# A two-layer decoder trunk on one core: a set of token sums one chunk pair later, and convolution steps held back while a seven-product chunk pair runs

## The chip, the core and the metric

The kernel runs on one core of a Trainium2 chip. The engines are named as the profile names them: PE multiplies matrices (PEld is its weight load), DVE is the vector engine, ACT the scalar engine, POOL and SP mostly issue DMAs. Each engine takes its instructions in a fixed order. The metric is the device time of one execution in microseconds (us), as a median over runs.

## The reference: what is computed

The trunk has two layers over 256 tokens of width 2048. Layer 0 mixes by gated linear attention, layer 1 by forgetting attention; both end in the channel mixer `conv_ffn`, which is where the change lies:

```
def causal_dwconv(u, w, b):
    s_ = u.shape[1]
    up = jnp.pad(u, ((0, 0), (CONV_WIDTH - 1, 0), (0, 0)))
    return w[0] * up[:, 0:s_] + w[1] * up[:, 1:s_ + 1] + w[2] * up[:, 2:s_ + 2] + b

def conv_ffn(h, w_up, conv_w, conv_b, w_down):
    u = causal_dwconv(h @ w_up, conv_w, conv_b)
    a, val = split_cols(u, [FFN_HIDDEN, FFN_HIDDEN])
    return (jax.nn.silu(a) * val) @ w_down
```

`w_up` is 2048 x 11264 and `w_down` 5632 x 2048, all in float32.

## The kernel before

**Products.** A float32 product is made of three passes of a rounded type: each operand is split into a high part (`hi`, a rounding copy) and a low part (`lo`, the rest), and hi x hi, lo x hi and hi x lo are added up in PSUM. Weights come from memory in units (`raw`, one DMA each, issued by SP). For every unit `split_unit` (lines 210 to 230) has ACT write `whi` (L229) and DVE write `wlo` (L230). There are four buffers each of `raw`, `whi` and `wlo`, so these engines can be at most four units ahead of PE.

**Wide panels.** `pair_steps` (from L363) runs one panel of 1024 output columns over chunks of 128 rows of the weight. An ordinary chunk is one unit: two blocks of tokens by two halves of columns, 12 matmuls of 128 x 512. Two neighbouring chunks whose token sums have been prepared are run as a **seven-product pair**: by a scheme of the Strassen kind the 2 x 2 x 2 block product takes seven products, 21 matmuls, instead of eight, 24. The pair has weights `ra` and `rb` (two DMAs into `raw2`), from which four weight blocks are split: `w1` (half of `ra`), `w2` (`rb`), and after four subtractions on DVE (L427 to L430) `w3` (`ra`, needs L427 and L428) and `w4` (`rb`, needs L429 and L430). `split_more` does the splits: ACT at L377, DVE at L378. The products are named p1 to p7; p1 uses w1, p2 and p3 use w2, p5 and p7 use w3, p6 and p4 use w4. When the last pair of a panel is done, `early` takes the finished banks out; its first step is an ACT copy of p1 (L1321 in the down projection, L1471 in the up projection), which waits for PE to finish p1, and in the down projection a DVE addition to the stream `x` (L485) follows on it.

**Token sums.** The sums of tokens and chunks that the seven products need are made by `token_sums` (four additions or subtractions on DVE, then a split on ACT and DVE, L671 and L672). For the up projection they are made once, for chunk 6 (`SEVEN_UP`), and for the first panel after each change of part also for chunk 11 (`SEVEN_MORE`). For the down projection they are made when the gated rows of certain chunks are finished: the table `SEVEN_DOWN` (L36) names chunk and buffer.

**Order of the work.** The 44 chunks of the hidden width go in three parts, 0 to 15, 16 to 27 and 28 to 43 (`PARTS`). An up panel (`up_pair`) makes four chunks of hidden rows; a down panel uses up the rows of a part. The up panels of a part come first, with one up panel of the next part ahead of the down panels. In the last part the first down panel is the one called `wide` below: it runs 12 of its 16 chunks, then three units of the narrow panel `f2`, then the last four chunks, whose hidden rows come last.

**Convolution steps.** The result of an up panel goes to memory and back in another layout (`far_away`, by POOL's DMAs) and is then convolved in small steps: 12 taps on ACT (L1383), two additions on DVE (L1390), the activation on ACT (L1396), the gating on DVE (L1403) and two splits (L515 on ACT, L516 on DVE). Each step has a cost in credits (0.5 per tap, 1.0 for an addition and so on, 10.2 for a half panel of two chunks). `pair_steps` yields once per chunk, twice after a seven-product pair; at each yield the driving loop calls `tick(share)`, which adds `share` credits and hands out due steps until the credit is used up. `drive` gives 1.3 credits per yield in up panels and in the other down panels, the loop over `wide` and `f2` gives 2.1. A step handed out is placed behind the latest weight split that was written (`issue_after(casts[-1])` or `lows[-1]`), and a scheduler that works on a model of the times then lays down the order on every engine.

Of the kernel before, what the change touches and what calls it, by code (L numbers as in the profile page):

```python
# [32 lines left out]
PARTS = ((0, 16), (16, 28), (28, 44))  # L33
RING = 20
SEVEN_UP = (6,)
SEVEN_DOWN = {4: 0, 10: 1, 20: 0, 32: 1}  # L36
SEVEN_MORE = 11


# [78 lines left out]
def _layout():  # L118

    where, off = {}, 0  # L120
    for key, _, kcs, cols, per in _panels():
        n = sum(c[1] for c in cols)
        units = []
        for u in range(0, len(kcs), per):
            units.append((off, kcs[u : u + per], n))
            off += P * per * n
        where[key] = units
    return where, off
# [17 lines left out]
def _trunk(ctx: ExitStack, tc: tile.TileContext, xt, xtok, memt, wp, wgu, gns, gfin, cnv, par, msk, out):  # L146
    nc = tc.nc
    where, _ = _layout()
# [232 lines left out]
    def pair_steps(units, src, sums, flip, pool, early, late):  # L381

        bank = {}
        fast, slow = ("p1", "p5", "p7", "p6"), ("p2", "p3", "p4", "x")
        accs, works = (slow, fast) if flip else (fast, slow)
        tags = {n: ("acc", 4) for n in accs}
        tags.update(zip(works, (("o", 1), ("s", 2), ("s", 2), ("t", 1))))
        begun = set()
        sums = dict(sums)
        n = len(units)  # L390
        plan = []
        k = 0
        while k < n:
            plan.append(k)
            k += 2 if k in sums else 1
        end = [k for k in plan if k in sums]

        def mm(name, x, w, last):
            if name not in bank:
                tag, bufs = tags[name]  # L400
                bank[name] = (pacc.tile([P, 512], F32, name="acc", tag="acc") if tag == "acc" else work(tag, bufs))
            r = TE.matmul(bank[name], x, w, start=name not in begun, stop=last)  # L402
            begun.add(name)
            return r

        def tok(k, b):
            return [src[k][:, part, b * P : (b + 1) * P] for part in range(2)]

        def three(name, x, w, last=False):
            for i, (a, b) in enumerate(((0, 0), (1, 0), (0, 1))):  # L410
                r = mm(name, x[a], w[b], last and i == 2)
            return r

        places = (("p2", 0, 0), ("p4", 1, 0), ("p3", 0, 1), ("x", 1, 1))
        for k in plan:
            if k in sums:
                with tc.high_priority(offset=AHEAD):
                    ra, rb = [pool.tile([P, NUNIT], F32, name="raw2", tag="raw2", bufs=2) for _ in range(2)]
                    with tc.issue_after(loads[-1].ins):
                        for t, (off, _, w) in ((ra, units[k]), (rb, units[k + 1])):  # L420
                            loads.append(nc.sync.dma_start(t, wp[off : off + P * w].rearrange("(p n) -> p n", p=P)))
                st = [[sums[k][:, part, j, :] for part in range(2)] for j in (3, 0, 1, 2)]
                done = k == end[-1]
                w1 = split_more(ra[:, :512], 512)
                w2 = split_more(rb, 1024)
                with tc.high_priority(offset=AHEAD):
                    V.tensor_tensor(ra[:, :512], ra[:, 512:], ra[:, :512], ALU.subtract)  # L427
                    V.tensor_tensor(ra[:, 512:], rb[:, 512:], ra[:, 512:], ALU.subtract)  # L428
                    V.tensor_tensor(rb[:, 512:], rb[:, 512:], ra[:, :512], ALU.subtract)  # L429
                    V.tensor_tensor(rb[:, :512], rb[:, :512], rb[:, 512:], ALU.subtract)  # L430
                three("p1", tok(k, 0), [t[:, :512] for t in w1], done)
                three("p2", tok(k + 1, 0), [t[:, :512] for t in w2])
                three("p3", st[3], [t[:, 512:] for t in w2])
                w3 = split_more(ra, 1024)
                three("p5", st[0], [t[:, :512] for t in w3], done)
                three("p7", st[2], [t[:, 512:] for t in w3], done)
                w4 = split_more(rb, 1024)
                three("p6", st[1], [t[:, 512:] for t in w4], done)
                last_mm.append(three("p4", tok(k + 1, 1), [t[:, :512] for t in w4]))
                if done:  # L440
                    early(bank)
                yield k
                k += 1
            else:
                w = split_unit(units[k])
                last = k == n - 1
                steps = [(low, *place) for low in range(2) for place in places]
                if last:
                    steps.sort(key=lambda t: places.index(t[1:]))
                for low, name, b, h in steps:  # L450
                    for part in range(2 - low):
                        r = mm(name, tok(k, b)[part], w[low][:, h * 512 : (h + 1) * 512], last and low == 1)
                    if last and low:
                        ends.append(r)
                        late(b, h, bank[name])
                last_mm.append(r)
            yield k
# [907 lines left out]
    def ffn(l, nx, h, m, ys, zs, landing, then, pool, temps, last=None, spare=None):  # L1365
        with tc.tile_pool(name=f"ffn{l}", bufs=1) as fp:
# [31 lines left out]
            def gated(j, s):  # L1398
# [6 lines left out]
                with tc.issue_after(lows[-1].ins):  # L1405
                    split(m, (j + s) % RING, r[:, s, :])
                    if s and j in SEVEN_DOWN:
                        sums[j] = held("dsum", SEVEN_DOWN[j])
                        token_sums(r, sums[j])
# [39 lines left out]
            def tick(share):  # L1449

                clock[0] += 1
                credit[0] = min(credit[0], 0.0) + share
                while returns and returns[0][0] <= clock[0] and not unread[returns[0][1]]:
                    _, slot, back, steps = returns.pop(0)
                    back()
                    unread[slot] = 12
                    waiting.extend(steps)
                while waiting and waiting[0][0] <= clock[0] and credit[0] > 0:
                    _, cost, step = waiting.pop(0)
                    credit[0] -= cost  # L1460
                    step()
# [27 lines left out]
                 9: lambda: nx.land(landing[1]), 11: nx.take}.get(k, int)()  # L1489
                tick(0)  # L1490

            def drive(steps, share=1.3):
                for _ in steps:
                    tick(share)

            up_sums = {k: input_sums(k) for k in SEVEN_UP}
            for k in up_pair(0):
# [22 lines left out]
            wide = down_pair(l, p, 0, src, {c - lo: t for c, t in sums.items()}, 0, pool, lambda: (temps(0), temps(1)), then)  # L1520
# [10 lines left out]
                f2 = panel_tm(("down", l, p, 2), src, third)  # L1531
                f3 = panel_tm(("down", l, p, 3), src, lambda b, a: (add_to(3)(b, a), then(3, b)))
            last_pair = hi - lo - 4
            for k in range(last_pair):
                next(wide)
                tick(2.1)
            getattr(then, "begin", int)()
            for u in range(3):
                f2(u)
                tick(2.1)  # L1540
            for _ in wide:
                tick(2.1)
            assert not waiting and not returns
            if l:
                for u in range(3, 8):
# [218 lines left out]
```

## Time and profile before

| what | value |
|---|---|
| runs, median (lowest to highest) | 2233.29 us (2229.81 to 2234.18), 3 runs |
| the profiled execution | 2230.85 us |
| its span, first to last instruction | 2229.1 us |
| PE busy | 2211.6 us, 10323 matmuls |
| DVE busy | 1789.9 us |
| ACT busy | 1418.9 us |
| granted PE clock over the span | 0.998 |

A row of the timeline is start, duration, engine, line, operation, the tiles written and read, their shape, a count and, in brackets, how long the engine was idle before it and who ended that. Matmuls are pipelined: a row's duration is longer than the time to the next start, so a loss on PE is read from starts. Names of tiles in the trace have no numbers; in the rows of the order they have.

### The profile page before, as it was taken

Reading aid. Unit: us, or ns where it says so; the run is one execution under the profiler, and the core shown is the slowest. Engines: PE = TensorE matmul, PEld = TensorE weight load, DVE = VectorE, ACT = ScalarE, POOL = GpSimd, SP = SyncE. Lnnn points to the kernel's source line nnn. Section 1 sums busy time; section 2 is a strip of 40 time slices with the busy share of each in tenths; the row PEclk is TensorE's granted clock in tenths of the full one; section 3 lists DMA queues with packets and bytes.
Section 4 is the critical chain, followed back from the end, with each engine's and each line's share of the span. In section 5 each row is a group of like instructions: output and inputs, shape, how many; then the busy total and the mean of one; then the engine's idle time right before and its main releaser. Section 6 shows DMA issues by size and latency. Waiting matters only on the chain.

```text
span 2229.1 us, 30049 instructions
## 1 busy us (share of the span) xinstructions
PE 2211.6 (99%) x10323; PEld 1851.9 (83%) x10323; DVE 1789.9 (80%) x2654; ACT 1418.9 (64%) x2257; POOL 136.0 (6%) x257
## 2 busy tenths in 40 slices
PE   9999999999999999999999999999999999999998
PEld 7888888888788888888788998888888888888876
DVE  7768977688887888898978569678888788888895
ACT  6655664556786567656765455455787657665874
POOL 0000000001100000001010000000001000100100
PEclk9999999999999999999999999999999999999999
DMA  9877567777778567667677867777677757766674
GB/s 348 249 224 224 193 186 245 253 233 242 228 234 267 183 221 238 227 233 233 222 247 250 237 194 249 228 240 249 210 241 238 252 175 246 232 241 209 226 259 146
DMA packets 165633, 515.47 MB, mean 231 GB/s; under 512 B 20700, under 2 KB 41832, under 8 KB 165480
## 3 DMA queue, kind: packets, MB, share of 16 engines
q1 hardware_dynamic: 148488, 461.36, 63.4%
q0 software_dynamic: 16416, 51.40, 7.5%
q8 instruction: 81, 1.33, 0.2%
q10 hardware_dynamic: 576, 0.79, 0.1%
q14 instruction: 72, 0.59, 0.1%
HBM read 469.68 MB, written 43.79 MB: 230 GB/s over the span
## 4 chain that ended last, share of the span: by engine, by line
PE 90%; issue 5%; ACT 2%; DMA 1%; DVE 1%; POOL 0%; SPq 0%; ACTq 0%; DVEq 0%; POOLq 0%
PE acc L333 26%; PE acc L402 25%; PE ps_s L402 13%; PE ps_o L402 7%; PE ps_t L402 6%; PE acc L305 3%; PE acc L260 3%; PE acc L363 2%; PE ps_s L333 2%; PE acc L258 1%; ACT tap L1383 1%; DMA raw<-wp 1%; ACT whi L229 1%; PE ps_s L1010 0%; DMA yzu<-far 0%
## 5 line engine op out<-in xcount | busy, mean ns | idle before, releaser
L230 DVE TENSOR_TENSOR wlo<-raw,whi 128x1024 fp32r<-128x1024 f32 (+4 forms) x739 | 874.1, 1194 | 289.0 <-ACT whi L229 261.9
L229 ACT ACTIVATE whi<-raw 128x1024 fp32r<-128x1024 f32 (+4 forms) x739 | 760.2, 1037 | 432.7 <-PE acc L333 151.2
L333 PE MATMUL acc<-whi,B 128*128 128x512 f32 (+3 forms) x1248 | 291.8, 370 | 0.0
L333 PEld LDWEIGHTS acc<-whi,B 128*128 128x128 f32 x1248 | 227.1, 188 | 28.1
L377 ACT ACTIVATE whi<-raw 128x1024 fp32r<-128x1024 f32 (+1 forms) x136 | 129.7, 954 | 188.8 <-PE ps_t L402 76.4
L378 DVE TENSOR_TENSOR wlo<-raw,whi 128x1024 fp32r<-128x1024 f32 (+1 forms) x136 | 147.6, 1087 | 65.5 <-ACT whi L377 60.7
L402 PE MATMUL acc<-whi,mix 128*128 128x512 f32 x764 | 195.4, 390 | 0.9 <-ACT whi L229 0.8
L402 PE MATMUL acc<-whi,B 128*128 128x512 f32 x750 | 193.0, 390 | 0.5 <-ACT whi L229 0.4
L402 PEld LDWEIGHTS acc<-whi,mix 128*128 128x128 f32 x764 | 143.0, 188 | 32.5 <-ACT whi L229 2.5
L402 PEld LDWEIGHTS acc<-whi,B 128*128 128x128 f32 x750 | 140.6, 188 | 31.0 <-ACT whi L229 1.6
L333 PE MATMUL acc<-wlo,B 128*128 128x512 f32 (+3 forms) x624 | 158.6, 369 | 0.0
L1383 ACT ACTIVATE tap<-yzu,cw 128x256 f32<-128x256 f32 x264 | 124.7, 530 | 4.0 <-DMA yzu<-far 4.0
L333 PEld LDWEIGHTS acc<-wlo,B 128*128 128x128 f32 x624 | 114.5, 188 | 14.6 <-DVE wlo L230 0.2
L1383 ACT ACTIVATE tap<-fvt,cw 128x256 f32<-128x256 f32 x264 | 124.7, 531 | 2.0 <-DMA fvt<-far 2.0
L402 PE MATMUL acc<-wlo,mix 128*128 128x512 f32 x382 | 107.8, 390 | 0.0
L402 PE MATMUL acc<-wlo,B 128*128 128x512 f32 x375 | 107.1, 390 | 0.0
L1390 DVE TENSOR_TENSOR tap<-tap,tap 128x1024 f32<-128x1024 f32 x88 | 106.7, 1213 | 0.0
L402 PE MATMUL ps_s<-whi,mix 128*128 128x512 f32 x386 | 105.2, 389 | 0.0
L402 PE MATMUL ps_s<-whi,B 128*128 128x512 f32 x342 | 94.3, 390 | 0.0
L402 PEld LDWEIGHTS ps_s<-whi,mix 128*128 128x128 f32 x386 | 72.5, 188 | 15.3
L402 PEld LDWEIGHTS acc<-wlo,mix 128*128 128x128 f32 x382 | 71.6, 188 | 15.3 <-DVE wlo L230 0.3
L402 PEld LDWEIGHTS acc<-wlo,B 128*128 128x128 f32 x375 | 70.3, 188 | 15.0 <-DVE wlo L230 0.3
(498 smaller groups left out, 3792.3 us busy)
## 6 DMA issues: line engine op xcount, KB each, us to landing
raw<-wp SPq DMA_DIRECT2D x743, 512.0 KB, 4.5
fvt<-far POOLq DMA_DIRECT2D x100, 128.0 KB, 4.6
raw<-wp SPq DMA_DIRECT2D x32, 384.0 KB, 3.5
far<-yu POOLq DMA_DIRECT2D x22, 512.0 KB, 5.5
far<-yzu POOLq DMA_DIRECT2D x22, 512.0 KB, 5.4
yzu<-far POOLq DMA_DIRECT2D x88, 128.0 KB, 5.2
raw<-wp SPq DMA_DIRECT2D x24, 388.0 KB, 5.2
x<-xtok SPq DMA_DIRECT2D x8, 512.0 KB, 7.3
```

What stands on the lines that cost most here:

```text
L229: casts.append(S.activation(hi[:, s], raw[:, s], AF.Copy))
L230: lows.append(V.tensor_tensor(lo[:, s], raw[:, s], hi[:, s].bitcast(F32), ALU.subtract))
L258: mm = TE.matmul(acc[p][c][:, :T], w[:, s], both[:, 0, :], start=False, stop=end and j == 3)
L260: mm = TE.matmul(acc[p][c], w[:, s], both, start=u == j == 0, stop=end and j == 3)
L305: mm = TE.matmul(acc[b][:, :n], src[kcs[j] - base][:, part, b * P : (b + 1) * P], w, start=u == 0 and low == part == j == 0, stop=u == end ...
L333: mm = TE.matmul(acc[b][:, :n], src[kc - base][:, part, b * P : (b + 1) * P], ready[low][:, j * n : (j + 1) * n], start=i == low == part = ...
L363: mm = TE.matmul(acc[b][:, :n], src[kc - base][:, part, b * P : (b + 1) * P], w, start=i == low == part == j == 0, stop=i == end and low = ...
L377: casts.append(S.activation(hi[:, :n], src, AF.Copy))
L378: lows.append(V.tensor_tensor(lo[:, :n], src, hi[:, :n].bitcast(F32), ALU.subtract))
L402: r = TE.matmul(bank[name], x, w, start=name not in begun, stop=last)
L1383: S.activation(by_run(taps[i][:, s, c, i:]), zs[slot][:, :, 2 * c + s], AF.Copy if i else AF.Identity, bias=0.0 if i else w[3], scale=w[2 ...
L1390: V.tensor_tensor(taps[0], taps[0], taps[n][:, :, :, :T], ALU.add)
```

## The change

Three edits. First, in the last part the token sums for a seven-product pair of the down projection are made for chunks 34 and 35 instead of 32 and 33, so that in `wide`, whose first chunk is 28, the pair is the seventh and eighth chunk instead of the fifth and sixth. Second, after a seven-product pair `pair_steps` yields -1 twice, and the loops give 0 credits for such a yield. Third, the credits at the other yields grow: 1.3 to 1.45 in `drive`, 2.1 to 2.4 in the loop over `wide`.

```
-SEVEN_DOWN = {4: 0, 10: 1, 20: 0, 32: 1}
+SEVEN_DOWN = {4: 0, 10: 1, 20: 0, 34: 1}
...
                 if done:
                     early(bank)
-                yield k
-                k += 1
+                yield -1
+                yield -1
+                continue
...
-            def drive(steps, share=1.3):
-                for _ in steps:
-                    tick(share)
+            def drive(steps, share=1.45):
+                for k in steps:
+                    tick(share if k >= 0 else 0.0)
...
-            for k in range(last_pair):
-                next(wide)
-                tick(2.1)
+            for _ in range(last_pair):
+                tick(2.4 if next(wide) >= 0 else 0.0)
             getattr(then, "begin", int)()
             for u in range(3):
                 f2(u)
-                tick(2.1)
+                tick(2.4)
             for _ in wide:
-                tick(2.1)
+                tick(2.4)
```

Both programs hold the same number of instructions on every engine; what moves is their order. Three places follow, in the first layer; the second layer shows the same moves. Line numbers behind the edits are higher by one in the changed program.

**DVE at the pair of `wide`.** `raw2` is the pair's weights, `wlo` a low part, `cv` and `moremv1` the gated rows of a convolution, `x0` the stream, `fvt` the copy that `early` makes of p1. Before:

```order
L230 TENSOR_TENSOR wlo_9976<-raw_9974,whi_9975 128x1024
L378 TENSOR_TENSOR wlo_9999<-raw2_9994,whi_9998 128x512
...
L1403 TENSOR_TENSOR cv_9970<-tap0_4575 128x512
L427 TENSOR_TENSOR raw2_9994<-raw2_9994 128x512
L516 TENSOR_TENSOR moremv1_4569<-cv_9970,moremv1_4569 128x256
L428 TENSOR_TENSOR raw2_9994<-raw2_9995,raw2_9994 128x512
L516 TENSOR_TENSOR moremv1_4569<-cv_9970,moremv1_4569 128x256
L485 TENSOR_TENSOR x0_79<-x0_79,fvt_4557 128x512
L429 TENSOR_TENSOR raw2_9995<-raw2_9995,raw2_9994 128x512
L378 TENSOR_TENSOR wlo_10021<-raw2_9994,whi_10020 128x1024
L430 TENSOR_TENSOR raw2_9995<-raw2_9995 128x512
L378 TENSOR_TENSOR wlo_10033<-raw2_9995,whi_10032 128x1024
```

In the changed program:

```order
L230 TENSOR_TENSOR wlo_10014<-raw_10012,whi_10013 128x1024
L378 TENSOR_TENSOR wlo_10035<-raw2_10030,whi_10034 128x512
L1404 TENSOR_TENSOR cv_9988<-tap0_4575 128x512
L378 TENSOR_TENSOR wlo_10039<-raw2_10031,whi_10038 128x1024
L427 TENSOR_TENSOR raw2_10030<-raw2_10030 128x512
L517 TENSOR_TENSOR moremv1_4569<-cv_9988,moremv1_4569 128x256 x2
L428 TENSOR_TENSOR raw2_10030<-raw2_10031,raw2_10030 128x512
L429 TENSOR_TENSOR raw2_10031<-raw2_10031,raw2_10030 128x512
L430 TENSOR_TENSOR raw2_10031<-raw2_10031 128x512
L378 TENSOR_TENSOR wlo_10057<-raw2_10030,whi_10056 128x1024
L486 TENSOR_TENSOR x0_79<-x0_79,fvt_4557 128x512
L378 TENSOR_TENSOR wlo_10069<-raw2_10031,whi_10068 128x1024
```

The subtractions now stand together, and the addition to `x0` behind them and behind the low part of w3. From the last L516 of the rows before (`moremk1`) to L427 the two programs have the same instructions, but for two more L230 in the changed one, those of the two chunks that now come ahead of the pair.

**ACT and PE at the same pair.** On ACT the copy of p1 stood ahead of the split of w3 (`whi_10020`); now it stands between w3 (`whi_10056`) and w4 (`whi_10068`). ACT before:

```order
L1396 ACTIVATE tap0_4575<-tap0_4575 128x2x256
L515 ACTIVATE moremv1_4569<-cv_9970 128x256 x2
L1321 ACTIVATE fvt_4557<-acc_10010 128x512
L377 ACTIVATE whi_10020<-raw2_9994 128x1024
L377 ACTIVATE whi_10032<-raw2_9995 128x1024
L229 ACTIVATE whi_10053<-raw_10052 128x1024
L229 ACTIVATE whi_10076<-raw_10075 128x1024
L229 ACTIVATE whi_10098<-raw_10097 128x1024
```

and PE and ACT in the changed program (PE first; `acc_10046` is p1, whose last matmul is the first row):

```order
L402 MATMUL acc_10046<-wlo_10035,A14_97 128x512
L402 MATMUL ps_o_9898<-whi_10038,A15_98 128x512
L402 MATMUL ps_s_9904<-whi_10038,dsum_9645 128x512 x2
L402 MATMUL ps_o_9898<-wlo_10039,A15_98 128x512
L402 MATMUL ps_s_9904<-wlo_10039,dsum_9645 128x512
L402 MATMUL acc_10060<-whi_10056,dsum_9645 128x512 x2
L402 MATMUL acc_10064<-whi_10056,dsum_9645 128x512 x2
L402 MATMUL acc_10072<-whi_10068,dsum_9645 128x512 x2
```

```order
L516 ACTIVATE moremv1_4569<-cv_9988 128x256 x2
L377 ACTIVATE whi_10056<-raw2_10030 128x1024
L1322 ACTIVATE fvt_4557<-acc_10046 128x512
L377 ACTIVATE whi_10068<-raw2_10031 128x1024
L229 ACTIVATE whi_10089<-raw_10088 128x1024
L229 ACTIVATE whi_10112<-raw_10111 128x1024
```

Five matmuls stand between the end of p1 and the first use of w3, and four more before the first use of w4.

**ACT behind the seven-product pair of an up panel** (the third up panel of the layer). Before, the taps of one convolution stand in one run ahead of the next chunk's `whi`:

```order
L377 ACTIVATE whi_5507<-raw2_5470 128x1024
L229 ACTIVATE whi_5536<-raw_5535 128x1024
L1383 ACTIVATE tap1_4576<-fvt_4557,cw_4573 128x4x2x32
L1383 ACTIVATE tap2_4577<-fvt_4557,cw_4573 128x4x2x32
L1383 ACTIVATE tap1_4576<-fvt_4557,cw_4573 128x4x2x32
L1383 ACTIVATE tap2_4577<-fvt_4557,cw_4573 128x4x2x32
L1383 ACTIVATE tap1_4576<-fvt_4557,cw_4573 128x4x2x32
L1383 ACTIVATE tap2_4577<-fvt_4557,cw_4573 128x4x2x32
L1383 ACTIVATE tap1_4576<-fvt_4557,cw_4573 128x4x2x32
L1383 ACTIVATE tap2_4577<-fvt_4557,cw_4573 128x4x2x32
L229 ACTIVATE whi_5556<-raw_5555 128x1024
```

In the changed program:

```order
L377 ACTIVATE whi_5507<-raw2_5470 128x1024
L229 ACTIVATE whi_5530<-raw_5529 128x1024
L1384 ACTIVATE tap1_4576<-fvt_4557,cw_4573 128x4x2x32
L1384 ACTIVATE tap2_4577<-fvt_4557,cw_4573 128x4x2x32
L1384 ACTIVATE tap1_4576<-fvt_4557,cw_4573 128x4x2x32
L1472 ACTIVATE fvt_4557<-ps_o_5485 128x512
L1473 ACTIVATE fvt_4557<-ps_o_5485,ny_4776 128x512
L229 ACTIVATE whi_5551<-raw_5550 128x1024
L1384 ACTIVATE tap2_4577<-fvt_4557,cw_4573 128x4x2x32
L1384 ACTIVATE tap1_4576<-fvt_4557,cw_4573 128x4x2x32
L1384 ACTIVATE tap2_4577<-fvt_4557,cw_4573 128x4x2x32
L229 ACTIVATE whi_5572<-raw_5571 128x1024
```

Three taps and the two copies of p1 (`ps_o_5485`) now stand ahead of the next `whi`, where eight taps stood, and each later `whi` has three taps ahead of it.

## The prediction

> **What bounds the kernel now.** I read the page first, for who is busy and what the last chain runs through.
>
> ```profile
> span 2229.1 us, 30049 instructions
> PE 2211.6 (99%) x10323; PEld 1851.9 (83%) x10323; DVE 1789.9 (80%) x2654; ACT 1418.9 (64%) x2257; POOL 136.0 (6%) x257
> PE 90%; issue 5%; ACT 2%; DMA 1%; DVE 1%; POOL 0%; SPq 0%; ACTq 0%; DVEq 0%; POOLq 0%
> ```
>
> PE bounds everything: the change removes no matmul, so it can only win back time in which PE stands still. The waits of PE's weight load tell how much that is, and the chain of waits what a matmul costs when nothing is late.
>
> ```profile
> PEld acc L402 <- ACT whi L377: 7.3, 6, 1.7
> PEld acc L402 <- ACT whi L229: 4.1, 8, 0.8
> PEld ps_o L402 <- ACT whi L229: 1.9, 9, 0.3
> PEld acc L402 <- DVE wlo L378: 1.5, 2, 0.8
> 458.02 16.32 PE acc L402 x72
> ```
>
> All of these are on L402, the wide panels that the change touches, and all are for split weights (columns: total, times, longest). They sum to 14.8 us, which is the most that better order could give. A matmul costs 16.32 / 72 = 0.2267 us, a chunk of 12 2.72 us. Next, in windows of 11 us, before and at the pair of `wide`, in both layers (columns behind the length: PE, PEld, DVE, ACT, POOL busy with counts, then the clock):
>
> ```profile
> 1082.00:1093.00 11.00, 11.00 (x50) 9.12 (x49) 11.00 (x14) 3.97 (x7) 3.29 (x6) 1.00 0.77 269
> 1093.00:1104.00 11.00, 8.50 (x35) 5.95 (x34) 8.88 (x13) 7.37 (x12) 2.18 (x4) 1.00 0.48 139
> 2129.07:2140.07 11.00, 11.00 (x50) 9.13 (x49) 11.00 (x15) 4.71 (x6) 1.51 (x3) 1.00 0.98 370
> 2140.00:2151.00 11.00, 8.41 (x35) 5.86 (x34) 9.82 (x15) 7.75 (x13) 4.04 (x8) 1.00 0.54 165
> ```
>
> The window with the pair holds 15 matmuls fewer: 15 x 0.2267 = 3.4 us lost in each layer. DVE is full (11.00 of 11) in the window ahead of it. The timelines of PE, ACT and DVE in the first layer say what was late:
>
> ```profile
> 1094.25 0.39 PE L402 MATMUL acc<-wlo,A 128*128 128x512 f32 x1
> 1094.72 0.40 PE L402 MATMUL ps_s<-wlo,dsum 128*128 128x512 f32 x1
> 1096.28 1.20 PE L402 MATMUL acc<-whi,dsum 128*128 128x512 f32 x4 [1.16 <-ACT whi L377]
> 1099.55 0.73 PE L402 MATMUL acc<-whi,dsum 128*128 128x512 f32 x2 [1.02 <-ACT whi L377]
> 1094.68 0.60 ACT L1321 ACTIVATE fvt<-acc 128x512 f32<-128x512 f32 x1 [1.42 <-PE acc L402]
> 1095.17 1.05 ACT L377 ACTIVATE whi<-raw 128x1024 fp32r<-128x1024 f32 x1
> 1098.44 1.06 ACT L377 ACTIVATE whi<-raw 128x1024 fp32r<-128x1024 f32 x1 [2.21 <-DVE raw L430]
> 1088.89 0.69 DVE L378 TENSOR_TENSOR wlo<-raw,whi 128x512 fp32r<-128x512 f32 x1
> 1087.76 1.22 DVE L230 TENSOR_TENSOR wlo<-raw,whi 128x1024 fp32r<-128x1024 f32 x1
> 1093.02 0.42 DVE L516 TENSOR_TENSOR moremv<-cv,moremv 128x256 fp32r<-128x256 f32 x1
> 1093.35 0.68 DVE L428 TENSOR_TENSOR raw<-raw,raw 128x512 f32<-128x512 f32 x1
> 1095.31 0.69 DVE L485 TENSOR_TENSOR x<-x,fvt 128x512 f32<-128x512 f32 x1 [0.94 <-ACT fvt L1321]
> 1095.92 0.68 DVE L429 TENSOR_TENSOR raw<-raw,raw 128x512 f32<-128x512 f32 x1
> 1097.66 0.68 DVE L430 TENSOR_TENSOR raw<-raw 128x512 f32<-128x512 f32 x1
> ```
>
> w3 is late because ACT held its split behind the copy of p1, which waits for PE; w4 because DVE held L429 and L430 behind the addition L485, which waits for that copy. Both are queues held up by their own consumer.
>
> **Part A, the pair two chunks later.** On PE the pair, and with it the need for w3, moves back by 24 matmuls, 24 x 0.2267 = 5.44 us. On DVE two more L230 stand ahead of L427; from the rows above one takes 1088.89 - 1087.76 = 1.13 us, so 2.26. DVE thus comes 5.44 - 2.26 = 3.18 us earlier by PE's clock. L428 has one more L516 (two in one row, 0.33 us, from 1093.02 to 1093.35) ahead of it, so 2.85 remain. I count now on the clock of before, where PE is ready for w3 at 1094.72 + 0.23 = 1094.95. L428 ended at 1094.03 and would end at 1091.2; the split of w3, no longer behind the copy, takes 1.05 us and is there at 1092.3, 2.6 us early. L429 and L430 follow directly, 0.61 us each (as from L485 to L429), and end at 1092.4 where L430 ended at 1098.34. Late next is w4, whose split stands behind the copy of p1. In the new order of PE the last matmul of p1 starts six steps before w3, at 1094.95 - 1.36 = 1093.59; the copy started 0.43 us after it (1094.25 to 1094.68) and held ACT for 0.49, so w4's split runs from 1094.51 to 1095.6. PE needs it four matmuls after w3 begins, at 1095.86. That is 0.26 us to spare: the loss goes, but narrowly. Bounds: nothing won if the DVE steps slip by as much as the pair (0), all of 3.4 us per layer. I take 3.4 x 2 = 6.8. The token sums themselves cost what they cost, later: the last of them before,
>
> ```profile
> L672 DVE TENSOR_TENSOR dsum<-cv,dsum x12: 674/680/686, 592.8 to 2090.7; 128x512 fp32r<-128x512 f32 x12
> ```
>
> starts at 2090.7, some 50 us ahead of the pair at 2141, and half an up panel (21 us) of delay is covered by this.
>
> **Part B, no steps while a pair runs.** This pays behind the pairs of up panels, where a run of taps stood ahead of the next chunk's split:
>
> ```profile
> 563.93 3.30 ACT L1383 ACTIVATE tap<-fvt,cw 128x256 f32<-128x256 f32 x8
> 567.13 1.05 ACT L229 ACTIVATE whi<-raw 128x1024 fp32r<-128x1024 f32 x1
> 566.77 1.07 PE L402 MATMUL acc<-wlo,B 128*128 128x512 f32 x4
> 570.21 1.20 PE L402 MATMUL acc<-wlo,B 128*128 128x512 f32 x4
> 1612.30 1.07 PE L402 MATMUL acc<-wlo,mix 128*128 128x512 f32 x4
> 1615.73 0.50 PE L402 MATMUL acc<-wlo,mix 128*128 128x512 f32 x1
> 1869.27 0.40 PE L402 MATMUL acc<-wlo,mix 128*128 128x512 f32 x1
> 1872.05 1.08 PE L402 MATMUL acc<-wlo,mix 128*128 128x512 f32 x4
> ```
>
> In the first two places PE starts 12 matmuls in 3.44 and 3.43 us where 2.72 would do, in the third 9 in 2.78 where 2.04 would: losses of 0.72, 0.71 and 0.74, together 2.2 us. Five of the eight taps, 5 x 0.41 (3.30 / 8) = 2.0 us, now stand behind the split, which covers 0.7; at the third place the split stands ahead of all taps. Bounds 0 and 2.2; I take 2.2. A place that stays is the second pair of a panel with two:
>
> ```profile
> 605.98 0.68 ACT L1472 ACTIVATE fvt<-acc,ny 128x512 f32<-128x512 f32 x1
> 606.54 1.06 ACT L377 ACTIVATE whi<-raw 128x1024 fp32r<-128x1024 f32 x1
> ```
>
> The order there has the copies ahead of w4 as before; I count nothing.
>
> **Part C, denser steps elsewhere.** The steps held back come out at 1.45 and 2.4 credits. In `drive` that is three taps per chunk, 1.05 + 3 x 0.41 = 2.3 us of ACT's 2.72: covered. In `wide` it is five, 1.05 + 5 x 0.41 = 3.1, over by 0.4 per chunk while 24 taps last, so 2 us per layer out of a lead that is up to four units (10.9 us). The narrowest place is the first split behind the ten taps after the pair, about 0.3 us to spare by the same count as above (two splits, ten taps, one split against the rest of the pair and two chunks). Bounds 0 and 2 us per layer; I take 0.3 per layer, 0.6, near the lower end since the order puts a split or two ahead of each run of taps. POOL's issues only change places; taps wait for them, and they come later now.
>
> **Sum.** 6.8 + 2.2 - 0.6 = 8.4 us won from the profiled execution's own 2230.85 us (span 2229.1 and 1.75 around it): 2222.5. The median of the runs shown, 2233.29, lies 2.4 above that execution; on its footing it would be 2224.9. I say 2223.5.
>
> **The rivals.** *The loss moves along with the pair.* For it: the same subtractions, gating and copy are in the queues, in nearly the old order, and w4 has 0.26 us to spare. Against it: the 5.44 against 2.26 us. Then only B is left: 2230.85 - 2.2 + 0.6 = 2229.3, no difference to be told.
>
> *The held-back steps make ACT the bound of the up panels.* Each pair now leaves two yields' worth of steps to the others; an up panel with one pair hands out 14 x 1.45 = 20.3 credits where it handed out 16 x 1.3 = 20.8 and needs 20.4, one with two pairs 17.4. Some taps take 0.59 us:
>
> ```profile
> 570.50 0.59 ACT L1383 ACTIVATE tap<-fvt,cw 128x256 f32<-128x256 f32 x1
> ```
>
> With those, a chunk costs ACT 1.05 + 3 x 0.59 = 2.82 us, more than PE's 2.72. If copies and scalings of a panel's end come on top and use up the lead, a chunk's 0.1 grows to 1 us per up panel; 20 such panels give 20, against 8.4 won: 2242. It decides from 13 us on, 0.65 a panel. Against it: PE loses nothing in most of these panels now, and the taps of 0.59 are a minority.
>
> *A slower clock goes with the stalls.* The rows of the windows show a granted clock of 1.00 with the stalls in them, so a stall costs its own length. The Trainium skill, "TensorE: Matmul & The Clock Gate" (A second HAM failure mode: psum-queue depth-cycling), tells of a kernel whose short idle times between groups of matmuls had the clock fall to half and return; by that rule each of the two stalls of about 1 us would halve the rate for some 3.4 us behind it and lose 1.7 us more, 3.4 us per pair of `wide`, an estimate by that page, and the change would give 8.4 + 6.8, 2215.7. The trace speaks against it.
>
> **Chances.** The forecast 0.76, the loss that moves along 0.12, ACT as the bound 0.09, the clock 0.03. About 0.2% (4.5 us) is what a measurement of this kernel tells from no change. Faster by more: 0.76 + 0.03, less 0.02 for a forecast that lands short, 0.77; within: 0.14; slower: 0.09. The range: at the low end the most that waits can give, 2230.85 - 14.8 = 2216; at the high end the loss that moves along on the median's footing, 2229.3 + 2.4 = 2232.
>
> **What would show it.** Right: the window of 11 us at the pair of `wide` holds 48 or 49 matmuls in both layers; PE's wait for L377 falls from 7.3 us to about 2; behind the third up panel's pair PE starts 12 matmuls in 2.72 us. Wrong in A: PE still waits for the pair's w3 or w4 by over 0.5 us. Wrong in B or C: new waits for L229 behind runs of taps. The prediction fails as a whole if waits for L229 grow by more than A wins.

## The result, and the profile after

| what | before | changed |
|---|---|---|
| median (lowest to highest) | 2232.15 us (2229.81 to 2234.18), 6 runs | 2222.82 us (2221.88 to 2224.22), 6 runs |
| the profiled execution | 2230.85 us | 2221.88 us |
| ratio, 95% interval | | 0.9958, 0.9946 to 0.9971 |

The change wins 9.3 us; 2223.5 was forecast. The total fits better than its terms, though, as the rest of this document shows. First the page of the changed kernel, its span, the busy times and the shares of the last chain:

```profile
span 2220.1 us, 30058 instructions
PE 2207.2 (99%) x10323; PEld 1853.8 (84%) x10323; DVE 1788.5 (81%) x2654; ACT 1418.8 (64%) x2257; POOL 136.1 (6%) x257
PE 95%; issue 2%; DVE 1%; DMA 1%; ACT 0%; POOL 0%; DVEq 0%; ACTq 0%; POOLq 0%
```

The work is the same; the chain has less in it that is not PE (10% before, 5% now). The waits of PE's weight load say which stalls went (total, times, longest):

```profile
PEld ps_t L596 <- DVE dg L594: 2.4, 1, 2.4
PEld ps_s L333 <- ACT whi L229: 1.2, 2, 0.7
PEld acc L402 <- ACT whi L229: 0.2, 1, 0.2
```

Of the 14.8 us on L402 in the prediction's four rows (15.4 with a fifth, 0.6 for L230) only 0.2 is left: every stall of both channel mixers is gone, the one that was to stay too. But L596 and L333 are new, and both lie behind the first layer. A window over the first channel mixer and the first weight loads of the attention behind that layer (starts of the first and the last of two) tell what that costs. Before the change:

```profile
457.00:1145.00 688.00, 684.89 (x3004) 562.74 (x3003) 584.70 (x723) 469.95 (x716) 60.88 (x113) 1.00 0.71 230
```

```profile
L506 PEld LDWEIGHTS ps_s<-mask,narrow x2: 141/142/143, 1257.6 to 1259.2; 128*128 128x128 f32 x2
```

and after it:

```profile
457.00:1145.00 688.00, 688.00 (x3028) 567.99 (x3027) 586.16 (x726) 472.39 (x718) 60.93 (x113) 1.00 0.72 232
```

```profile
L507 PEld LDWEIGHTS ps_s<-mask,narrow x2: 141/142/142, 1255.1 to 1256.7; 128*128 128x128 f32 x2
```

In the mixer PE now does 24 matmuls more in the same 688 us, 24 x 0.2267 = 5.4 us won. At the attention only 1257.6 - 1255.1 = 2.5 us are left of it, so about 3 us were given back in between. The spans differ by 9.0, so the second layer, with nothing like that behind it, keeps 9.0 - 2.5 = 6.5. Where they were given back (two windows, then the timeline of PE, DVE and ACT):

```profile
1170.00:1180.00 10.00, 9.73 (x44) 7.74 (x43) 10.00 (x31) 10.00 (x23) 0.56 (x1) 1.00 0.63 208
1200.00:1210.00 10.00, 8.00 (x37) 6.33 (x36) 9.63 (x15) 4.25 (x6) 0.00 (x0) 1.00 0.74 230
```

```profile
1190.53 1.06 ACT L229 ACTIVATE whi<-raw 128x1024 fp32r<-128x1024 f32 x1 [4.22 <-DMA raw<-wp]
1191.62 1.23 DVE L230 TENSOR_TENSOR wlo<-raw,whi 128x1024 fp32r<-128x1024 f32 x1 [2.79 <-ACT whi L229]
1203.46 0.38 PE L596 MATMUL ps_t<-dg,onesr 128*128 128x256 f32 x1 [2.00 <-DVE dg L594]
```

DVE and ACT are both full from 1170 to 1180 us: the last additions to `x`, their squares for the norm and the splits of the next stage's inputs come together there. They were nearly as full before the change, when PE lost nothing by it:

```profile
1170.00:1180.00 10.00, 10.00 (x44) 8.10 (x44) 10.00 (x26) 9.17 (x20) 0.00 (x0) 1.00 0.51 165
```

PE, 5 us earlier than before, now meets this. Afterwards DVE's steps of the norm (L561 to L564, L594) stand between low parts that wait for late weights, and the matmul that spreads the norm (L596) waits 2.0 us for them.

At the wide pair the changed kernel looks as forecast. Windows of 11 us ahead of and at the pair in the first layer, and at the pair in the second:

```profile
1085.00:1096.00 11.00, 11.00 (x50) 9.13 (x49) 10.93 (x15) 4.57 (x7) 2.74 (x5) 1.00 0.92 260
1096.00:1107.00 11.00, 11.00 (x50) 8.98 (x49) 10.15 (x13) 9.80 (x17) 2.19 (x4) 1.00 0.58 198
2143.00:2154.00 11.00, 11.00 (x49) 8.88 (x48) 10.88 (x13) 10.39 (x18) 1.90 (x4) 1.00 0.60 188
```

49 or 50 matmuls stand at the pair where 35 stood. The timeline of the pair in the first layer shows the room:

```profile
1094.09 0.69 DVE L428 TENSOR_TENSOR raw<-raw,raw 128x512 f32<-128x512 f32 x1
1094.89 1.06 ACT L377 ACTIVATE whi<-raw 128x1024 fp32r<-128x1024 f32 x1 [2.37 <-DVE raw L428]
1097.20 0.60 ACT L1322 ACTIVATE fvt<-acc 128x512 f32<-128x512 f32 x1 [1.24 <-PE acc L402]
1097.69 1.05 ACT L377 ACTIVATE whi<-raw 128x1024 fp32r<-128x1024 f32 x1
1098.16 1.56 PE L402 MATMUL acc<-whi,dsum 128*128 128x512 f32 x6
```

The split of w3 ends at 1095.95, and PE takes it at 1098.16: 2.2 us early (2.6 forecast). The split of w4 ends at 1098.74, and PE takes it four matmuls into the last row, at 1098.16 + 0.91 = 1099.07: 0.33 us early (0.26 forecast).

### The profile page after: what moved, and what is told of

It reads as the page before. It is cut to its first block, busy times and chain, and to the rows that moved or that the text cites. A ratio compares the mean times of both kernels' runs of the same rounds, so it can differ in the third digit from the quotient of the medians.

```text
span 2220.1 us, 30058 instructions
## 1 busy us (share of the span) xinstructions
PE 2207.2 (99%) x10323; PEld 1853.8 (84%) x10323; DVE 1788.5 (81%) x2654; ACT 1418.8 (64%) x2257; POOL 136.1 (6%) x257
## 4 chain that ended last, share of the span: by engine, by line
PE 95%; issue 2%; DVE 1%; DMA 1%; ACT 0%; POOL 0%; DVEq 0%; ACTq 0%; POOLq 0%
PE acc L402 30%; PE acc L333 23%; PE ps_s L402 15%; PE ps_o L402 7%; PE ps_t L402 7%; PE acc L305 3%; PE acc L260 3%; PE acc L363 2%; PE acc L258 1%; PE ps_s L333 1%; DVE wlo L230 0%; PE ps_s L1011 0%; DMA raw<-wp 0%; DMA fvt<-far 0%; PE ps_o L686 0%
## 5 line engine op out<-in xcount | busy, mean ns | idle before, releaser
L230 DVE TENSOR_TENSOR wlo<-raw,whi 128x1024 fp32r<-128x1024 f32 (+4 forms) x739 | 876.8, 1196 | 256.6 <-ACT whi L229 232.6
L229 ACT ACTIVATE whi<-raw 128x1024 fp32r<-128x1024 f32 (+4 forms) x739 | 760.4, 1037 | 447.4 <-PE acc L333 166.3
L333 PE MATMUL acc<-whi,B 128*128 128x512 f32 (+3 forms) x1248 | 292.0, 370 | 0.0
L377 ACT ACTIVATE whi<-raw 128x1024 fp32r<-128x1024 f32 (+1 forms) x136 | 129.8, 954 | 190.7 <-PE acc L402 75.5
L333 PEld LDWEIGHTS acc<-whi,B 128*128 128x128 f32 x1248 | 227.1, 188 | 28.0
L402 PE MATMUL acc<-whi,mix 128*128 128x512 f32 x764 | 194.6, 389 | 0.0
L402 PE MATMUL acc<-whi,B 128*128 128x512 f32 x750 | 193.0, 389 | 0.0
L402 PEld LDWEIGHTS acc<-whi,mix 128*128 128x128 f32 x764 | 143.3, 188 | 30.2 <-ACT whi L229 0.2
L402 PEld LDWEIGHTS acc<-whi,B 128*128 128x128 f32 x750 | 140.8, 188 | 29.6
L333 PE MATMUL acc<-wlo,B 128*128 128x512 f32 (+3 forms) x624 | 158.6, 369 | 0.0
L333 PEld LDWEIGHTS acc<-wlo,B 128*128 128x128 f32 x624 | 114.6, 188 | 14.5
L402 PE MATMUL acc<-wlo,mix 128*128 128x512 f32 x382 | 107.5, 389 | 0.0
L402 PE MATMUL acc<-wlo,B 128*128 128x512 f32 x375 | 107.3, 389 | 0.0
L402 PE MATMUL ps_s<-whi,mix 128*128 128x512 f32 x386 | 106.1, 389 | 0.0
L402 PE MATMUL ps_s<-whi,B 128*128 128x512 f32 x342 | 93.5, 389 | 0.0
L402 PEld LDWEIGHTS ps_s<-whi,mix 128*128 128x128 f32 x386 | 72.5, 188 | 15.3
L402 PEld LDWEIGHTS acc<-wlo,mix 128*128 128x128 f32 x382 | 71.7, 188 | 15.0
L402 PEld LDWEIGHTS acc<-wlo,B 128*128 128x128 f32 x375 | 70.4, 188 | 14.7
```

Of the source, the lines that this page charges most:

```text
L229: casts.append(S.activation(hi[:, s], raw[:, s], AF.Copy))
L230: lows.append(V.tensor_tensor(lo[:, s], raw[:, s], hi[:, s].bitcast(F32), ALU.subtract))
L333: mm = TE.matmul(acc[b][:, :n], src[kc - base][:, part, b * P : (b + 1) * P], ready[low][:, j * n : (j + 1) * n], start=i == low == part = ...
L377: casts.append(S.activation(hi[:, :n], src, AF.Copy))
```

## The experiments

All ratios are to the kernel before, run on the same chip; the last digits are 95% intervals. Pair, holding back and credits are the three parts of the change.

| label | pair | held back | credits | median us | ratio |
|---|---|---|---|---|---|
| pair_only | 34 | no | old | 2229.10 | 0.9986 (0.9977 to 0.9995) |
| shares_only | 32 | no | new | 2238.43 | 1.0027 (1.0016 to 1.0038) |
| pair_shares | 34 | no | new | 2233.47 | 1.0006 (0.9997 to 1.0015) |
| hold_only | 32 | yes | new | 2231.05 | 0.9992 (0.9983 to 1.0001) |
| hold_old | 34 | yes | old | 2224.23 | 0.9966 (0.9954 to 0.9979) |
| after_again | 34 | yes | new | 2222.31 | 0.9953 (0.9938 to 0.9967) |

**The pair alone.** `SEVEN_DOWN` with 34 for 32, all else as before.

> The kernel before with the token sums for chunk 34 instead of 32 and nothing else: steps are handed out while a pair runs, with 1.3 and 2.1 credits, as before. Theory (the parts add up, and the later pair is worth its own stall): PE stands still about 3.4 us less in the window of the wide pair in each layer, the span falls by 6 to 7 us, to about 2222.5, and the median to about 2225.5; the losses behind the up panels' pairs stay. Rival (holding the steps back is what cures the wide pair, moving it only carries the loss along): PE's wait for L377 stays at 6 to 7 us, only its place is 5.4 us later, and the median stays within 1 us of before.

3.1 us faster, half of what was expected. Its waits, and two rows at the panel ahead of `wide`:

```profile
PEld acc L402 <- ACT whi L229: 4.7, 8, 0.8
PEld acc L333 <- DVE wlo L230: 1.8, 1, 1.8
PEld acc L402 <- ACT whi L377: 1.1, 2, 0.6
```

```profile
1058.38 3.30 ACT L1383 ACTIVATE tap<-fvt,cw 128x256 f32<-128x256 f32 x8
1062.68 1.65 PE L402 MATMUL acc<-whi,B 128*128 128x512 f32 x6 [0.39 <-ACT whi L229]
```

The wait for L377 fell from 7.3 to 1.1: no loss at the wide pair in either layer (what is left lies in up panels), so the theory holds there. But a run of eight taps now stands ahead of a split in the last up panel, as it did in other panels, and the first layer again gives back nearly all it won: its attention starts at 1257.3, 0.3 us before the old kernel's.

**Held back and denser, but the pair at 32.** The changed kernel with 32 for 34.

> The changed kernel with the token sums back at chunk 32: steps are held back while a pair runs and the credits are 1.45 and 2.4, but the wide pair stands where it stood. Theory: PE still waits for w3 and w4 of the wide pair, 3 us or more in each layer; what is won is the rest of the feed-forward stages. By the sum of the prediction that is 2.2 - 0.6 = 1.6 us, by the trace of the changed kernel up to 14.0 - 6.8 = 7.2 us, less what a new wait behind the first layer's channel mixer takes: a median between 2225 and 2231. Rival (holding back cures the wide pair as well): no wait for L377 is left, and the median is within 1 us of the changed kernel's 2222.8.

As in the theory the wide pair still loses, and more than before; the median, 2231.05 us, lies at the upper edge of what was expected (windows of 2 us, then the timeline of PE):

```profile
1092.00:1094.00 2.00, 0.57 (x3) 0.13 (x1) 1.23 (x3) 1.86 (x4) 0.00 (x0) 1.00 1.01 313
1094.00:1096.00 2.00, 1.28 (x5) 0.76 (x5) 2.00 (x4) 0.29 (x1) 0.00 (x0) 0.99 0.08 33
1096.00:1098.00 2.00, 1.47 (x3) 0.75 (x4) 0.82 (x2) 1.44 (x2) 1.93 (x4) 0.50 0.29 59
1098.00:1100.00 2.00, 2.00 (x6) 1.52 (x6) 2.00 (x3) 2.00 (x3) 0.24 (x1) 0.50 0.73 203
1100.00:1102.00 2.00, 2.00 (x6) 1.61 (x5) 2.00 (x3) 2.00 (x6) 0.00 (x0) 0.50 0.35 117
1102.00:1104.00 2.00, 2.00 (x8) 1.59 (x8) 1.48 (x3) 2.00 (x6) 0.00 (x0) 0.81 0.93 258
```

```profile
1094.34 1.20 PE L402 MATMUL acc<-whi,dsum 128*128 128x512 f32 x4 [1.77 <-ACT whi L377]
1098.69 1.05 PE L402 MATMUL ps_s<-whi,A 128*128 128x512 f32 x2
1102.10 0.63 PE L402 MATMUL acc<-wlo,dsum 128*128 128x512 f32 x1
```

31 matmuls in 12 us, where 12 / 0.2267 = 53 fit: 5.0 us lost. Part of it is no wait at all. Behind the wait of 1.77 us the granted clock falls to 0.50, and from 1098.69 to 1102.10 eight matmuls take 3.41 us instead of 1.81: 1.6 us for the clock in these alone. The kernel before, with waits of at most 1.2 us there, kept 1.00. Not every execution of hold_only loses so much: of its eleven, the six with a mean clock of 0.996 took 2231.05 to 2232.10 us, the five with 0.997 to 0.999 took 2226.34 to 2230.06. A good part of what the pair at 32 costs here is the clock.

**The credits alone**, 1.45 and 2.4 at every yield; and **pair and credits**, with steps handed out while a pair runs.

> The kernel before with credits of 1.45 and 2.4 at every yield, pair and hand-outs as before. Theory (denser steps cost a little): the stalls at the wide pair stay, those behind the up panels' pairs stay or grow, the median is 0 to 2 us above before. Rival (the denser hand-out, not the holding back, took away the small waits of the feed-forward stages): the median falls by 2 to 7 us.

> Pair moved and credits of 1.45 and 2.4, but steps handed out while a pair runs. Theory (the denser steps hurt at the wide pair only while it stands early, on a DVE that is full): the wide pair's stalls of 4 to 6 us per layer, which the denser steps alone have, go, the stalls behind the up panels' pairs stay, and the median is about 2226 to 2229. Rival (moving the pair and the denser steps each cost or win what they do alone): 2238.4 - 3.2, about 2235.

The denser steps alone cost 6 us, against 0 to 2 expected: the weight load waits 11.1 us for L377, and behind the wide pair's stall the clock falls here too (0.50 from 1100 to 1106 us). From 1101.80 to 1106.07 us ten matmuls take 4.27 us instead of 2.27, and from 2154.12 to 2157.46 eight take 3.34 instead of 1.81: of the 8.7 us between the two profiled spans, some 3.5 are the clock in these rows alone. With the pair moved the cost falls by 5 us, nearer to the rival than to the 9 to 12 of the theory, and 1.3 us over before remain, not to be told from none. The stall at the wide pair is gone here too, as in the theory; but 5.1 us are lost behind the first layer, and the up panels lose more than before. Holding the steps back is what makes the denser credits harmless: from pair_shares to the changed kernel it is 1.0006 to 0.9953, 11 to 12 us.

**Old credits.** `share=1.3` and 2.1 in the changed kernel.

> The changed kernel with the old credits, 1.3 and 2.1: the pair is moved and steps are held back, but nothing makes up for those held back. By the sum of the prediction the denser steps cost 0.6 us, so the median is about 2222.2. Rival one (the denser steps cost as much as they do alone, 6 us): about 2217. Rival two (what is held back has to come out somewhere, and at the old credits it comes too late for its panel): PE waits for gated rows or token sums, or the rest is handed out in a run at a panel's end, and the median is 2224 or more.

0.9966 against 0.9953 in another run of the changed kernel, with intervals that overlap: 2 to 3 us slower, if it is more than nothing. The credits' 6 us of cost (rival one) are not there, and the sign is that of rival two. A part of it is seen: in `wide` PE's weight load waits for low parts of hidden rows that now come too late, and by starts PE loses 0.5 us there in each layer.

```profile
PEld ps_o L402 <- DVE mix L517: 1.1, 2, 0.5
```

**The queue held up by the copy.** The kernel before, but in `early` of the down projection:

```
+            with tc.issue_after(casts[-1].ins):
                 S.activation(t0, bank["p1"], AF.Copy)
+            with tc.issue_after(lows[-1].ins):
                 add_to(f)(0, t0)
```

> The kernel before, but for the copy of p1 at the last pair of a down panel, which ACT now does behind the split of w4, and the addition to x that follows on it, which DVE does behind w4's low part. Pair, hand-outs and credits as before. Theory (the stall is two queues held up by the copy that waits for PE): without moving the pair the stall of 3.4 us shrinks to about 0.7 in each layer (0.2 for w3's split and 0.5 for its low part, since L428 still ends at the same time), so the span falls by about 5.4 us and PE's wait for L377 from 7.3 to under 2 us. Rival (DVE is simply too late by its work, the place of the copy makes no difference): the wait for L377 stays above 5 us and the time within 1 us of before.

0.9980 (0.9971 to 0.9989), a median of 2227.94: 4.4 us faster, with pair and credits untouched. PE and the two waits that are left at the pair:

```profile
1094.58 1.20 PE L402 MATMUL acc<-whi,dsum 128*128 128x512 f32 x4 [0.15 <-ACT whi L377]
1096.25 0.73 PE L402 MATMUL acc<-whi,dsum 128*128 128x512 f32 x2 [0.46 <-ACT whi L377]
```

PE's waits for L377 of 1.16 and 1.02 us before have become 0.15 and 0.46. By starts (from start to start, less 0.2267 us a matmul) the wide pair wins 2.2 us in the first layer and 2.1 in the second, out of 3.4 each. So about two thirds of the stall were the order of two queues, as the prediction said. The rest is work on DVE that ends late, as the rival had it: with the copy out of the way, ACT waits for the subtractions ahead of both splits:

```profile
1093.47 1.06 ACT L377 ACTIVATE whi<-raw 128x1024 fp32r<-128x1024 f32 x1 [0.89 <-DVE raw L428]
1095.13 1.06 ACT L377 ACTIVATE whi<-raw 128x1024 fp32r<-128x1024 f32 x1 [0.60 <-DVE raw L430]
```

A later pair cures both parts. The weight load's wait for L377 was 4.3 us, not under 2, and behind the first layer some 2.7 us were given back here as well.

**The same edit on hold_only**, to see whether its larger stall is the same thing.

> hold_only with the edit of copy_behind: pair at chunk 32, steps held back, denser credits, and the copy of p1 and the addition behind w4's split and low part. Theory (the 6 us that hold_only loses at the wide pair in each layer are the queues held up by that copy, and half of it the clock that falls behind a stall of 2 us): the stall shrinks to about 1 us per layer, the granted clock stays at 1.00 there, and the median is 2221 to 2225, as good as moving the pair. Rival (the pair at 32 is too early for DVE's work whatever the order, and only a later pair cures it): over 2 us are lost at the pair in each layer and the median stays above 2227.

0.9961 (0.9948 to 0.9974), 2223.22 us: 7 us better than hold_only and level with the changed kernel within the intervals. The stall does shrink and the clock at the wide pair stays at 1.00; by starts PE still loses 2.2 us there in the first layer and 1.3 in the second, so 1 us per layer was too little. The profiled execution is the slowest of the five (2228.23 us, the others 2222.52 to 2224.70): it loses 5.4 us behind the first layer, around a wait of 2.0 us with the clock at half behind it.

**Later still.** 36 for 34.

> The changed kernel with the token sums for chunk 36 instead of 34, another 5.44 us later. Theory (at 34 nothing is late any more at the wide pair, so more room wins nothing): no wait of PE at the pair, the median within 1 us of 2222.8. Rival one (the margin at w4, a third of a microsecond, is too narrow in other executions): 1 to 2 us faster. Rival two (the token sums come too late for their products): PE waits for dsum, slower by over 1 us.

0.9979 (0.9971 to 0.9988), 2227.11 us: about 5 us slower than the changed kernel, as rival two had it, but not by its mechanism: no wait for a token sum shows. On ACT a run of taps stands ahead of w3's split:

```profile
1098.91 3.29 ACT L1384 ACTIVATE tap<-fvt,cw 128x256 f32<-128x256 f32 x8
1103.71 1.99 ACT L377 ACTIVATE whi<-raw 128x1024 fp32r<-128x1024 f32 x2
1104.80 1.46 PE L402 MATMUL acc<-whi,dsum 128*128 128x512 f32 x5 [1.30 <-ACT whi L377]
```

So room on DVE does not decide alone; what is handed out in the yields just ahead of the pair counts as well. The larger part of the loss lies behind the first layer, some 7 us by starts against 3, with waits of up to 2.4 us and a clock of 0.50 behind the last.

**What is given back behind the first layer.** Three trials on the changed kernel. The first hands out the splits of the last landed input later (behind unit 7 of the second panel instead of unit 5); the last two units of the first two panels then multiply with what those buffers held before.

> The changed kernel, but in the key projection behind the first layer the splits of the last landed input (hook at unit 5 of the second panel) are handed out at unit 7. In the order DVE then does the last steps of the norm and the two L594 ahead of the low parts of B_111 to B_114 instead of between and behind them. Theory (the time lost behind the first layer is DVE's queue ahead of L594): PE's wait of 2.0 us for dg goes, the span falls by about 2 us and the median to about 2220.7. Rival (weights are what comes late there): PE waits for a split of the same stage instead, and the median stays within 0.7 us of 2222.8.

2223.08 us, 0.9962 (0.9949 to 0.9974). L594 comes 2.6 us earlier, but the order puts L596 earlier on PE as well, and PE still waits 2.0 us. The second holds L596 itself back, beside a plain repeat:

```
+                    with tc.issue_after(behind.ins) if behind is not None else nullcontext():
                         self.spread = TE.matmul(pr[:, :T], onesr, dg, ...)
...
-            two_tm([fk(0), fk(1)], 8, 2, {(1, 2): nx.row,
+            two_tm([fk(0), fk(1)], 8, 2, {(1, 2): nx.col, (0, 7): lambda: nx.row(last_mm[-1]),
```

> The changed kernel, but the two matmuls that spread the norm behind the first layer (L596) are held behind the last matmul of the seventh unit pair of the key projection's first panel, about 20 matmuls or 4.5 us later on PE; the order on DVE stays as in the changed kernel. Theory (PE loses time there because this matmul stands ahead of others that could run, while its input is late on DVE): PE's wait of 2.0 us for dg goes, the span falls by about 2 us and the median to about 2220.5. Rival (the weights of that stage are late, and PE meets the next late split instead): waits for L229 or L230 of 1.5 to 2 us stand in its place, the median stays within 0.7 us of the changed kernel run beside it.

> The changed kernel again, beside the other two on one chip. Every theory: 2222 to 2224 us; in its profile PE waits for dg about 2 us behind the first layer, and whether the granted clock falls behind that wait tells if a wait of this length decides it by itself.

The repeat of the changed kernel has the same span, 2220.1, with the loss in other places: 1.1 us for L594 and 1.5 us for L230, where the first profile had 2.0 and none. The wait of 2 us that was expected did not come, so this run doesn't tell what such a wait does to the clock. row_behind loses the 1.1 and keeps the 1.5; at 2221.44 us, 0.9947 (0.9933 to 0.9961), it is 0.9 us below the repeat, not to be told from it. Its windows show what is left, 39 and 42 matmuls where 44 fit:

```profile
1170.00:1180.00 10.00, 9.04 (x39) 6.85 (x38) 10.00 (x25) 10.00 (x25) 0.56 (x1) 1.00 0.52 146
1180.00:1190.00 10.00, 9.47 (x42) 7.52 (x41) 8.65 (x20) 2.38 (x3) 2.50 (x5) 1.00 0.73 236
```

The third takes work out of DVE's queue there, on top of row_behind:

```
             def query_input(i):
-                split_turned(hq, i, (*stash, spare[1])[i // 4], "mix1")
+                with tc.issue_after(lows[-1].ins):
+                    split_turned(hq, i, (*stash, spare[1])[i // 4], "mix1")
```

> row_behind with one edit more: the splits of the query projection's inputs (L527 and L529, 24 of these on DVE between 1165 and 1180 us in the changed kernel's trace, and needed only some 40 us later) are each held behind the latest low part, so that DVE does them in the key projection, where it has room. Theory (the time given back behind the first layer, 2.6 us in row_behind, is DVE's queue, filled with work that nobody needs yet): PE's waits for L230 in that stretch go, the window from 1170 to 1180 us holds 44 to 46 matmuls, and the median is 2218.5 to 2219.5. Rival one (the weights themselves come too late there): the waits stay, the median is within 0.7 us of row_behind's 2221.4. Rival two (the delayed splits crowd the key projection): waits of 1 us and more between 1205 and 1260 us, no gain or a loss.

2222.12 us, 0.9948 (0.9935 to 0.9962): nothing won. DVE has room (8.43 of 10 us busy in that window), PE's waits for L230 are gone, and in their place stands one for ACT:

```profile
PEld acc L333 <- ACT whi L229: 3.6, 3, 2.6
```

In the order on ACT the high parts of the moved splits and the squares for the norm still stand ahead of the weights, and these squares wait for the additions to `x` that follow on PE's last matmuls. Neither theory nor rivals had that. How to win these 3 us stays open.

## Why the prediction was right, point by point

**Part A, 6.8 us.** At its place it is right: both stalls are gone, in the changed kernel and in pair_only, with the room for w3 and w4 within 0.4 us of what was worked out. The mechanism, two queues held up by the copy, is shown by copy_behind for about two thirds of the stall; the rest is DVE's lateness, which the 3.18 us of the prediction cover as well. What failed is that the term was read as a gain in the total: alone it gives 3.1 us, since pair_only has a new stall in the last up panel of each layer and the first layer gives back the rest.

**Part B, 2.2 us.** The runs of eight taps ahead of a split are gone; behind the third up panel's pair 12 matmuls go from start to start of these rows in 569.30 - 566.55 = 2.75 us (2.72 forecast, 3.44 before):

```profile
566.55 1.09 PE L402 MATMUL acc<-wlo,B 128*128 128x512 f32 x4
567.48 1.98 PE L402 MATMUL acc<-whi,B 128*128 128x512 f32 x8
569.30 1.07 PE L402 MATMUL acc<-wlo,B 128*128 128x512 f32 x4
```

The term was too small: from pair_only to hold_old, which differ in it alone, it is 0.9986 to 0.9966, about 4.5 us, though the ends of their intervals just meet; with the new credits, from pair_shares to the changed kernel, it is 11 to 12. "A place that stays" did not stay: the copies still stand ahead of w4, but PE does not wait there, and wins 0.5 us by starts in the first layer. And the step of leaving out what A does to other panels missed the tap run of pair_only, which B also removes.

**Part C, -0.6 us.** Wrong in sign, if anything: with the steps held back, the denser credits win 2 to 3 us at most, since hidden rows come in time. That they are harmless depends wholly on B; alone they cost 6.0 us, beyond the 4 us that the bounds allowed for two layers, and part of that is the clock, for which the term has nothing.

**The sum, 8.4 us.** It treated three parts as separate. The table says otherwise: pair alone 3.1, the other two alone 1.8 (the interval reaches to none), all three 9.4 to 10.5. A good part of that gap is the clock, which falls behind the wide pair's stalls in hold_only and stays at 1.00 there in the changed kernel. The starts of the n-th matmul in both traces, compared place by place, say what made up the 9.0 us between the spans. The wide pairs win 3.3 and 3.5 us, 6.8 as forecast. The up panels win 2.0 and 3.0, together 5.0, where B and C have 2.2 - 0.6 = 1.6. And 3.0 us, for which there was no term, come back behind the first layer. So A's size was right at its place, and that the other two errors nearly cancel is luck. The low end of the range left out the fifth row of waits on L402, 0.6 us, which changes nothing here.

**The rivals.** The loss that moves along: not at the pair, but 3 us of it did, a stage later, into queues that were nearly full before and cost nothing while PE was late; neither row_behind nor query_row got rid of it. ACT as the bound of the up panels: no; the wait for L229 on L402 fell from 6.0 to 0.2. In pair_36 and pair_only, though, taps on ACT do decide single places. The slower clock: not for the stalls of the kernel before, but the claim that "a stall costs its own length" holds only for these. In hold_only and shares_only it failed at both wide pairs, behind waits of 1.8 us; the last section says what sets these apart.

## What to carry to other kernels

A stall whose releaser is itself queued behind work that waits for PE can be met by order, in either of two ways: more room, which took all of it away here, or the waiting copy put behind the splits, which took two thirds. Edits that hand out the same work at other times are not additive: price them together, at each place where a queue is full, and look at the stage behind the one that gets faster. A matmul placed for a modelled ready time costs PE when its input is late, since nothing behind it on PE started in the meantime (2.0 us at L596).

## What the runs showed of the hardware that was not expected

The granted clock answers to a wait of under 2 us, and not each time. The traces say more about when. In all fourteen of them every change of the granted clock lies a whole number of stretches of 3.4133 us behind the first change (in hold_only it falls at 1095.95 and at 2143.84 us, 307 such stretches apart), and the seven spells at half rate between the start and PE's last matmul last one stretch, 3.41 us, or two, 6.83 us. The rows show such stretches: take_late with its wait of 1.98 us for L594, then the changed kernel with its wait of 2.00 us, then the wide pair of the kernel before.

```profile
1198.65:1202.07 3.42, 1.44 (x7) 1.10 (x7) 3.35 (x9) 1.44 (x2) 0.00 (x0) 1.00 0.55 181
1202.07:1205.48 3.41, 3.41 (x9) 2.64 (x8) 2.52 (x3) 1.06 (x1) 0.00 (x0) 0.50 0.84 259
```

```profile
1198.49:1201.90 3.41, 2.98 (x14) 2.12 (x12) 3.41 (x12) 2.30 (x4) 0.00 (x0) 1.00 0.49 154
1201.90:1205.31 3.41, 1.84 (x9) 1.59 (x10) 3.38 (x7) 1.74 (x3) 0.00 (x0) 1.00 0.72 208
1205.31:1208.73 3.42, 3.42 (x17) 2.82 (x16) 3.08 (x4) 1.65 (x2) 0.00 (x0) 1.00 0.86 264
```

```profile
1095.71:1099.13 3.42, 1.93 (x6) 0.97 (x6) 2.63 (x4) 1.21 (x2) 2.18 (x4) 1.00 0.27 63
```

In take_late the whole wait falls into one stretch; PE is busy for 1.44 us of it, and the clock is at half for the next. In the changed kernel the wait is divided between two stretches with 2.98 and 1.84 us of work, and the clock stays at 1.00. In the kernel before, parts of three shorter waits leave 1.93 us, and it stays too. In the stretches ahead of the seven falls PE is busy for 0.98 to 1.67 us. No other stretch up to PE's last matmul has less than 1.64 (query_row, a wait of 2.2 us, also divided), and the next has 1.84. So these traces fit a share of work in a stretch, with the border at about half, and not the length of a wait; none of the runs varies the one without the other, so this is not shown. The Trainium skill, "TensorE: Matmul & The Clock Gate" (What's actually happening), has PE's activity judged in a free-running window of 3413 ns; the traces agree, with 3.4133 us. Its advice in the same page (Why this matters for your kernels), to avoid idle gaps over about 3 us, is too mild by these rows: a wait of 1.8 us that fell whole into one stretch was enough (shares_only, first layer).
